# Ten experts per layer loaded in single buffers, and the last experts and the final norm reordered, in a two-layer mixture-of-experts trunk

## The chip, the core and the metric

The kernel runs on one core of one Trainium2 chip, in one launch. The metric is the device time of one execution in microseconds (us). The profile is one execution on the chip; its times count from the span's first instruction. Engines are named as in the profile: PE (TensorE; PEld is its weight load), DVE (VectorE), ACT (ScalarE), POOL (GpSimd) and SP (SyncE, which issues nearly all DMAs here).

## What is computed

Two layers on 256 tokens of width 1024, in float32. Layer 0 mixes tokens by forgetting attention, layer 1 by retention. Each is followed by a mixture of experts: a router picks 2 of 32 experts per token, and the result is added to the residual stream `h`. After layer 1 comes a last RMS norm.

```python
for i in range(DEPTH):                       # DEPTH = 2
    hn = rms_norm(h, norm_mix[i])
    h = h + (forgetting_attention if i == 0 else retention)(hn, ...)
    hn = rms_norm(h, norm_ffn[i])
    h = h + hier_moe(hn, ...)                # sum over 2 chosen experts of gate * expert(hn)
return rms_norm(h, norm_final)
# expert e: a, b = split(x @ w_gu[e]); (silu(a) * b) @ w_down[e]     w_gu[e] 1024x1024, w_down[e] 512x1024
```

Each layer reads all 32 experts' weights: 4 MiB of `w_gu` and 2 MiB of `w_down` for each, 192 MiB a layer.

## The kernel before, in words

**Stages.** `phase_a` is layer 0's attention with its router logits, `phase_moe(0, ...)` its experts, `phase_c` layer 1's retention, `phase_moe(1, ...)` its experts, and `final_norm` is a generator whose parts are run from inside the last expert.

**Weight buffers.** All large weights go through 26 slots of SBUF, 1 MiB each (128 partitions x 2048 float32). `Stream` holds a list `todo` of loads in the order of their use. `pump` issues from SP, in that order, as long as there are free slots: a load of 1 MiB takes one slot (`one`), a load of 2 MiB takes two neighbours `u` and `u ^ 1` (`two`), and where no such pair is free nothing more is issued. A slot comes free where the program calls `done` (or `give`); the DMA instruction then waits on the chip for the last reader of its slot. SP takes its instructions in order, so a load that waits holds up those behind it. `reserve` keeps slots back for buffers that the next stage will claim.

**Pieces of an expert.** `pieces(e)` says whether an expert's weights come in 1 MiB loads (four for `w_gu`, two for `w_down`) or in 2 MiB loads (two and one). Before, experts 0 to 4 (`FINE = 5`) and expert 31 come in the finer form. Expert 31's `w_down` comes in four loads of 512 KiB, one per 256 output columns (`quarter`).

**One expert.** Tokens of four experts (a group `g4`, with `e4` 0 to 3 inside it) are gathered together, 32 rows for each. `first_product` (L1037) runs four parts of 16 matmul records each (L1047); after the parts that end a load it calls `done`. For experts 29 and 30 (`WARM = 29`) each part is followed by `keep_warm(2)`: products of a matrix of ones with itself whose result nobody reads (L533). Then ACT takes the silu (L1056), DVE multiplies (L1057) and transposes (L1064), and the second product (L1075) follows, whose result DVE and ACT copy to `y4` (L1088, L1090). After `e4 == 1` `scatter_mats` prepares the group's scatter matrix; after `e4 == 2` the next group's rows are gathered (L970); at the end of a group four `scatter` products (L1101) add `y4` to the accumulators `sums[t, n]`, four PSUM banks (two halves of the tokens, two halves of the columns), which collect all groups of a layer.

**The end of a layer.** After expert 30 the program runs `keep_warm(8)` and `last_mats` (L1104: one DVE product, two transposes L1113, two thin products L1115, two DVE evictions). `last_expert` then scatters the three finished experts of the group in four products, one before and three between the parts of expert 31's first product, and runs `keep_warm(4)` after the fourth part. Second product and scatter of expert 31 go in four column pieces: `second_product(i)` (PE L1132, DVE L1135) and `scatter_piece(i)` (PE L1143), after which DVE adds the accumulator to `h` (L1145). Between them run the parts of the next stage (`between`): in layer 0 the start of `phase_c`, in layer 1 `piece(i)` of `final_norm`. The order is a string of steps, w for a second product, s for a scatter piece, b for a part of the next stage; in layer 1 it is `w0 w1 s0 w2 s1 b0 w3 s2 b1 s3 b2 b3`.

**The last norm.** `piece(i)` squares a quarter of `h` with row sums (ACT L387; for the last quarter DVE takes one of two, L385), and multiplies `h` by the gain into `fin` (POOL for quarters 0 to 2, DVE for quarter 3, L1525). After the last squares, `row_rstd` (L394 to L396) makes the factor, ACT and DVE scale the halves of `fin`, and SP stores four pieces of 256 KiB.

Of the kernel before, what the change touches and what calls it, by code (L numbers as in the profile page):

```python
# [16 lines left out]
AF = mybir.ActivationFunctionType  # L17
# [4 lines left out]
P = 128  # L22
# [8 lines left out]

FINE = 5
AHEAD = 3
# [194 lines left out]
def trunk(ctx, tc, x, fox_w_in, fox_b_f, fox_w_out, ret_w_in, ret_gn_gain, ret_w_out,  # L228
# [149 lines left out]

    def squares(i, junk, c=None, n=512, dve=False):

        c = 512 * i if c is None else c
        for t in range(2):
            a = h[:, t, c:c + n]
            if dve and t:
                V.scalar_tensor_tensor(junk[:, n:2 * n], a, 1.0, a, ALU.mult, ALU.mult, accum_out=ss[:, i, t:t + 1])  # L385
            else:
                A.activation(junk[:, 0:n], a, AF.Square, accum_out=ss[:, i, t:t + 1])  # L387

# [529 lines left out]


    def phase_moe(l, g, reserve_after, ahead, before_last, between):  # L920
        gi = 1 + 2 * l
# [144 lines left out]
        def expert(e, e4, xg, y4, after_part):  # L1066
            gg, gTt = first_product(e, e4, xg, after_part)
            turned(gg, gTt)
            by = bank("o")
            n = 4 // pieces(e)  # L1070
            for j in range(4):
                key = "wd", l, e, j // n
                w = st.get(key)
                for nb in range(4):
                    mm(by[32 * nb:32 * nb + 32, 0:256], gTt[:, 32 * j:32 * j + 32],  # L1075
                       w[:, j % n, 256 * nb:256 * nb + 256], start=j == 0, stop=j == 3, skip_group_check=True)
                if j % n == n - 1:
                    st.done(key)
                if j % 2 and e >= WARM:
                    keep_warm(2, "sc")  # L1080
            if e == 0:
                third()
                y4 = w2["y4"][0]
            for nb in range(4):
                o = y4[32 * e4:32 * e4 + 32, 256 * nb:256 * nb + 256]
                i = by[32 * nb:32 * nb + 32, 0:256]
                if nb % 2:
                    A.activation(o, i, AF.Copy)  # L1088
                else:
                    V.tensor_copy(o, i)  # L1090


        sums = {}

# [25 lines left out]
        def last_expert(xg, y4):  # L1120
            scatter(y4, 0, 96)
            gg, gTt = first_product(31, 3, xg, lambda part: scatter(y4, part + 1, 96) if part < 3 else None)
            keep_warm(4, "sc")
            turned(gg, gTt)
# [14 lines left out]
            def scatter_piece(i):  # L1139
                c = quarter(l, i)  # L1140
                for t in range(2):
                    b = sums[t, c.start // 512][:, c.start % 512:c.start % 512 + 256]
                    mm(b, w2["sm"][:, P * t:P * t + P], yd[:, i, :], start=False, stop=True, skip_group_check=True)  # L1143
                    hv = h[:, t, c]
                    V.tensor_tensor(hv, hv, b, ALU.add)  # L1145

# [14 lines left out]
        for g4 in range(8):  # L1161
            xg = g.xg if g4 % 2 == 0 else w2["xg"]
            for e4 in range(4):
# [5 lines left out]
                if e4 == 1:  # L1169
                    scatter_mats(g4)  # L1170
                if e == 2:
                    st.reserve += 2
# [5 lines left out]
                if e in ahead:  # L1178
                    before_last()
                if e == 30:  # L1180
                    keep_warm(8, "sc")
                    last_mats()
            if g4 < 7:
# [320 lines left out]
    def final_norm():  # L1504
# [14 lines left out]
        def piece(i):  # L1519
            c = quarter(1, i)  # L1520
            squares(i, junk, c.start, 256, dve=i == 3)
            if i == 3:
                row_rstd(4)
            for t in range(2):
                (G if i < 3 else V).tensor_tensor(fin[:, t, c], h[:, t, c], gain[:, c], ALU.mult)  # L1525

# [4 lines left out]
        for n in range(2):  # L1531
# [3 lines left out]
            A.activation(fin[:, 0, c], fin[:, 0, c], AF.Copy, scale=rstd[:, 0:1])  # L1535
            nc.sync.dma_start(out[0, 0:P, c], fin[:, 0, c])
        yield
# [39 lines left out]
```

## Time and profile before

| | us |
|---|---|
| median of 3 runs | 1263.21 |
| lowest and highest run | 1260.52, 1263.24 |
| the profiled execution, its own time | 1264.12 |
| its span, first to last instruction | 1262.4 |
| PE busy | 992.3 (79%) |
| DVE busy | 416.7 (33%) |
| DMA, mean over the span | 366 GB/s of 462 MB moved |

The table's busy times are sums over the whole span. The kernel has stages with different limits: PE is busy nearly all the time in the two mixer stages (about 0 to 160 us and 600 to 805 us), and the DMA engines in the two expert stages (about 172 to 600 us and 817 to 1244 us). So the stretch in which a change acts says what it is worth, not the sums. A row of a window gives, for a stretch, each engine's busy time with its number of instructions, the granted TensorE clock as a share of 2.4 GHz (0.50 is 1.2 GHz), the share of time that the 16 DMA engines were busy, and what they moved.

### The profile page before, as it was taken

What the parts mean: (1) busy time and instruction counts of PE and PEld (TensorE: products, weight loads), DVE (VectorE), ACT (ScalarE), POOL (GpSimd) and SP (SyncE); (2) the same over time, 40 slices, a digit from 0 to 9 for tenths busy, and PEclk for the clock granted to TensorE, in tenths of its full rate; (3) what the DMA queues carried; (4) which work ended last, traced back from release to release, by engine and by line L of the source; (5) the groups of instructions that cost most, each with busy time, mean ns of one, the idle gap of its engine ahead of it and who ended that gap; (6) DMA issues with size and microseconds to landing.
All of it is one profiled execution on the core that took longest, in us unless ns stands there. A gap on an engine that the chain in (4) does not pass through costs nothing. (4 is left out here: it accounts for less than half of the span.)

```text
span 1262.4 us, 21607 instructions
## 1 busy us (share of the span) xinstructions
PE 992.3 (79%) x9279; PEld 638.7 (51%) x9279; DVE 416.7 (33%) x931; ACT 317.0 (25%) x670; POOL 46.8 (4%) x55
## 2 busy tenths in 40 slices
PE   8999986777576666678999999977766666676787
PEld 8888853343232333234989888743432333233344
DVE  6776741211111111112777776421111111111113
ACT  5665521111010010101554665311110101010111
POOL 2000000000000000000223100000000000000001
PEclk9999999999797979789999999999978787877879
DMA  9966878999999999999982678779999999999994
GB/s 327 336 253 228 307 295 342 429 424 428 427 427 427 428 427 426 428 428 393 371 318 77 242 258 336 276 295 421 427 427 426 427 428 428 426 428 426 428 424 175
DMA packets 70088, 462.22 MB, mean 366 GB/s; under 512 B 8401, under 2 KB 13281, under 8 KB 41570
## 3 DMA queue, kind: packets, MB, share of 16 engines
q1 hardware_dynamic: 69568, 460.70, 90.0%
q8 instruction: 75, 1.23, 0.4%
q14 instruction: 27, 0.22, 0.0%
q10 hardware_dynamic: 418, 0.07, 0.0%
HBM read 459.70 MB, written 1.05 MB: 365 GB/s over the span
## 5 line engine op out<-in xcount | busy, mean ns | idle before, releaser
L1047 PE MATMUL sc<-slot,slot 128*32 128x256 f32 x4096 | 281.2, 426 | 57.5 <-DMA slot<-in_expert_w_gu_dram 54.2
L1047 PEld LDWEIGHTS sc<-slot,slot 128*32 128x32 f32 x4096 | 137.8, 120 | 188.4 <-issue 81.3
L1075 PE MATMUL o<-slot,slot 128*32 128x256 f32 x1984 | 145.5, 441 | 105.3 <-DMA slot<-in_expert_w_down_dram 59.6
L1075 PEld LDWEIGHTS o<-slot,slot 128*32 128x32 f32 x1984 | 72.5, 123 | 173.6 <-issue 85.6
L1057 DVE TENSOR_TENSOR slot<-slot,sc 128x128 f32<-128x128 f32 x64 | 23.8, 371 | 396.6 <-ACT slot L1056 396.6
L467 DVE SCALAR_TENSOR_TENSOR slot<-slot,gT,slot 128x512 fp32r<-128x512 f32 x160 | 125.0, 801 | 50.0 <-ACT slot L456 48.6
L500 PE MATMUL acc<-slot,slot 128*128 128x256 f32 x960 | 125.1, 287 | 0.9 <-ACT slot L456 0.4
L1090 DVE COPY slot<-o 32x256 f32<-32x256 f32 x124 | 51.8, 418 | 215.4 <-PE o L1075 188.2
L456 ACT ACTIVATE slot<-slot,gT 128x512 fp32r<-128x512 f32 x160 | 111.4, 718 | 36.2 <-PE acc L500 15.1
L500 PEld LDWEIGHTS acc<-slot,slot 128*128 128x128 f32 x960 | 118.6, 192 | 3.3 <-ACT slot L456 0.7
L1088 ACT ACTIVATE slot<-o 32x256 f32<-32x256 f32 x124 | 46.5, 375 | 292.6 <-DVE slot L1090 292.6
L1056 ACT ACTIVATE slot<-sc 128x128 f32<-128x128 f32 x64 | 17.7, 277 | 383.9 <-PE sc L1047 383.9
L512 PE MATMUL acc<-slot,slot 128*128 128x512 f32 x256 | 102.5, 400 | 0.0
L513 PE MATMUL acc<-slot,slot 128*128 128x512 f32 x256 | 100.1, 391 | 1.8 <-DVE slot L467 1.8
L514 PE MATMUL acc<-slot,slot 128*128 128x512 f32 x256 | 100.1, 391 | 0.0
L970 PE MATMUL sc<-h,slot 128*128 128x512 f32 x112 | 69.3, 778 | 33.5 <-DVE slot L959 33.5
L1101 PE MATMUL acc<-slot,slot 128*128 128x512 f32 (+1 forms) x128 | 60.9, 611 | 13.2 <-ACT slot L1088 13.2
L970 PEld LDWEIGHTS sc<-h,slot 128*128 128x128 f32 x112 | 26.5, 247 | 73.0 <-issue 73.0
L513 PEld LDWEIGHTS acc<-slot,slot 128*128 128x128 f32 x256 | 48.2, 188 | 11.6 <-DVE slot L467 2.7
L514 PEld LDWEIGHTS acc<-slot,slot 128*128 128x128 f32 x256 | 48.1, 188 | 10.2
L512 PEld LDWEIGHTS acc<-slot,slot 128*128 128x128 f32 x256 | 48.2, 188 | 9.3 <-issue 0.3
L978 DVE TENSOR_TENSOR slot<-pt,gT 128x512 f32<-128x512 f32 x28 | 19.4, 692 | 93.1 <-PE pt L977 93.1
(236 smaller groups left out, 763.2 us busy)
## 6 DMA issues: line engine op xcount, KB each, us to landing
slot<-in_expert_w_gu_dram SPq DMA_DIRECT2D x104, 2048.0 KB, 39.1
slot<-in_expert_w_down_dram SPq DMA_DIRECT2D x52, 2048.0 KB, 39.1
slot<-in_expert_w_gu_dram SPq DMA_DIRECT2D x46, 1024.0 KB, 7.5
slot<-in_ret_w_in_dram SPq DMA_DIRECT2D x24, 1024.0 KB, 14.2
slot<-in_expert_w_down_dram SPq DMA_DIRECT2D x20, 1024.0 KB, 7.7
slot<-in_fox_w_in_dram SPq DMA_DIRECT2D x15, 1024.0 KB, 13.3
slot<-in_ret_w_out_dram SPq DMA_DIRECT2D x8, 1024.0 KB, 8.8
slot<-in_fox_w_out_dram SPq DMA_DIRECT2D x4, 1024.0 KB, 15.5
```

Of the source, the lines that this page charges most:

```text
L456: A.activation(wh, w, AF.Copy, scale=1.0 if g is None else g)
L467: V.scalar_tensor_tensor(wl, w, g, wh, ALU.mult, ALU.subtract)
L500: mm(o, w[:, P * j:P * j + P], x[:, k, :], start=first and k == 0 and j % 2 == 0, stop=last and k == 7, skip_group_check=True)
L512: mm(banks[t], xh[:, q], wh, start=first and k == ks[0], stop=False)
L513: mm(banks[t], xh[:, q], wl, start=False, stop=False)
L514: mm(banks[t], xl[:, q], wh, start=False, stop=last and k == ks[-1])
L970: mm(b, o[:, t, :], h[:, t, 512 * n:512 * n + 512], start=t == 0, stop=t == 1)
L1047: mm(bgu[32 * j:32 * j + 32, 0:256].rearrange("p (two f) -> p two f", two=2), xg[:, kk, 32 * e4:32 * e4 + 32], wv[:, :, P * j:P * j + P], ...
L1075: mm(by[32 * nb:32 * nb + 32, 0:256], gTt[:, 32 * j:32 * j + 32], w[:, j % n, 256 * nb:256 * nb + 256], start=j == 0, stop=j == 3, skip_gr ...
L1088: A.activation(o, i, AF.Copy)
L1090: V.tensor_copy(o, i)
L1101: mm(sums[t, n], w2["scm"][0:rows, P * t:P * t + P], y4[0:rows, 512 * n:512 * n + 512], start=start, stop=False, skip_group_check=True)
```

## The change

- `FINE` goes from 5 to 10: experts 5 to 9 of both layers are loaded 1 MiB at a time into single slots.
- In experts 29 and 30 the second `keep_warm(2)` of the second product goes; after expert 30 `keep_warm(8)` goes, and `last_mats` moves to after expert 29.
- In `last_expert` the scatters of the finished experts stand one after each part of the first product; `keep_warm(4)` goes.
- In layer 1, after expert 24, four products of the identity with `h` add `h` to the accumulators. The DVE additions L1145 are left to layer 0. `final_norm` reads the accumulators in place of `h`: ACT squares all, DVE does all products with the gain, POOL none.
- Of the four stores of the result two are issued from ACT's queue.

```diff
--- before.py
+++ after.py
@@ -29,7 +29,7 @@
 CAP = 32
 NSLOT = 26
 
-FINE = 5
+FINE = 10
 AHEAD = 3
 
 WARM = 29
@@ -376,15 +376,10 @@
     rstd = small("rstd", 2)
 
 
-    def squares(i, junk, c=None, n=512, dve=False):
-
-        c = 512 * i if c is None else c
+    def squares(i, junk):
+
         for t in range(2):
-            a = h[:, t, c:c + n]
-            if dve and t:
-                V.scalar_tensor_tensor(junk[:, n:2 * n], a, 1.0, a, ALU.mult, ALU.mult, accum_out=ss[:, i, t:t + 1])
-            else:
-                A.activation(junk[:, 0:n], a, AF.Square, accum_out=ss[:, i, t:t + 1])
+            A.activation(junk[:, 0:512], h[:, t, 512 * i:512 * i + 512], AF.Square, accum_out=ss[:, i, t:t + 1])
 
     def row_rstd(parts=2):
 
@@ -917,6 +912,8 @@
         return g
 
 
+    hsum = {}
+
     def phase_moe(l, g, reserve_after, ahead, before_last, between):
         gi = 1 + 2 * l
         r = g.room
@@ -1076,7 +1073,7 @@
                        w[:, j % n, 256 * nb:256 * nb + 256], start=j == 0, stop=j == 3, skip_group_check=True)
                 if j % n == n - 1:
                     st.done(key)
-                if j % 2 and e >= WARM:
+                if j == 1 and e >= WARM:
                     keep_warm(2, "sc")
             if e == 0:
                 third()
@@ -1090,7 +1087,7 @@
                     V.tensor_copy(o, i)
 
 
-        sums = {}
+        sums = hsum if l else {}
 
         def scatter(y4, i, rows=P):
 
@@ -1118,9 +1115,7 @@
             V.tensor_scalar(gs, cst[:, C_NB:C_NB + 4], b[:, T:T + 1], None, ALU.mult)
 
         def last_expert(xg, y4):
-            scatter(y4, 0, 96)
-            gg, gTt = first_product(31, 3, xg, lambda part: scatter(y4, part + 1, 96) if part < 3 else None)
-            keep_warm(4, "sc")
+            gg, gTt = first_product(31, 3, xg, lambda part: scatter(y4, part, 96))
             turned(gg, gTt)
             yd = g.xg.rearrange("p (i n) q -> p i n q", i=4).rearrange("p i n q -> p i (n q)")
 
@@ -1141,8 +1136,9 @@
                 for t in range(2):
                     b = sums[t, c.start // 512][:, c.start % 512:c.start % 512 + 256]
                     mm(b, w2["sm"][:, P * t:P * t + P], yd[:, i, :], start=False, stop=True, skip_group_check=True)
-                    hv = h[:, t, c]
-                    V.tensor_tensor(hv, hv, b, ALU.add)
+                    if l == 0:
+                        hv = h[:, t, c]
+                        V.tensor_tensor(hv, hv, b, ALU.add)
 
             what = {"w": second_product, "s": scatter_piece, "b": between}
             for o in (("w0 w1 s0 s1 b0 w2 b1 s2 w3 b2 s3 b3 b4") if l == 0 else
@@ -1168,6 +1164,8 @@
                 expert(e, e4, xg, w2["y4"][g4 % 2] if e else None, start if e == 0 else lambda part: None)
                 if e4 == 1:
                     scatter_mats(g4)
+                    if g4 == 7:
+                        last_mats()
                 if e == 2:
                     st.reserve += 2
                 if e4 == 2 and g4 < 7:
@@ -1177,9 +1175,10 @@
                     st.reserve = reserve_after
                 if e in ahead:
                     before_last()
-                if e == 30:
-                    keep_warm(8, "sc")
-                    last_mats()
+                if l and e == 24:
+                    for t, n in sums:
+                        mm(sums[t, n], ident, h[:, t, 512 * n:512 * n + 512], start=False, stop=False,
+                           skip_group_check=True)
             if g4 < 7:
                 for i in range(4):
                     scatter(w2["y4"][g4 % 2], i)
@@ -1518,11 +1517,13 @@
 
         def piece(i):
             c = quarter(1, i)
-            squares(i, junk, c.start, 256, dve=i == 3)
+            hs = [hsum[t, c.start // 512][:, c.start % 512:c.start % 512 + 256] for t in range(2)]
+            for t in range(2):
+                A.activation(junk[:, 0:256], hs[t], AF.Square, accum_out=ss[:, i, t:t + 1])
             if i == 3:
                 row_rstd(4)
-            for t in range(2):
-                (G if i < 3 else V).tensor_tensor(fin[:, t, c], h[:, t, c], gain[:, c], ALU.mult)
+            for t in (1, 0):
+                V.tensor_tensor(fin[:, t, c], hs[t], gain[:, c], ALU.mult)
 
         for i in range(3):
             piece(i)
@@ -1533,7 +1534,7 @@
             V.tensor_scalar(fin[:, 1, c], fin[:, 1, c], rstd[:, 1:2], None, ALU.mult)
             nc.sync.dma_start(out[0, P:2 * P, c], fin[:, 1, c])
             A.activation(fin[:, 0, c], fin[:, 0, c], AF.Copy, scale=rstd[:, 0:1])
-            nc.sync.dma_start(out[0, 0:P, c], fin[:, 0, c])
+            A.dma_start(out[0, 0:P, c], fin[:, 0, c])
         yield
 
     g = phase_a()
```

The order in which instructions stand moves at three places. SP's queue in layer 0, from the last loads of expert 4 (the names are slots; `128x2048` fills one, `128x4096` a pair); before:

```order
L166 DMA slot_28_991<-in_expert_w_down_dram 128x2048
L166 DMA slot_25_143<-in_expert_w_down_dram 128x2048
L166 DMA slot_38_1971<-in_expert_w_gu_dram 128x4096
L166 DMA slot_39_2047<-in_expert_w_gu_dram 128x4096
L166 DMA slot_40_2057<-in_expert_w_down_dram 128x4096
L166 DMA slot_41_2102<-in_expert_w_gu_dram 128x4096
L166 DMA slot_42_2112<-in_expert_w_gu_dram 128x4096
```

and with the change:

```order
L166 DMA slot_28_991<-in_expert_w_down_dram 128x2048
L166 DMA slot_25_143<-in_expert_w_down_dram 128x2048
L166 DMA slot_8_117<-in_expert_w_gu_dram 128x2048
L166 DMA slot_4_100<-in_expert_w_gu_dram 128x2048
L166 DMA slot_5_107<-in_expert_w_gu_dram 128x2048
L166 DMA slot_29_1403<-in_expert_w_gu_dram 128x2048
L166 DMA slot_30_1405<-in_expert_w_down_dram 128x2048
L166 DMA slot_31_1431<-in_expert_w_down_dram 128x2048
L166 DMA slot_16_125<-in_expert_w_gu_dram 128x2048
L166 DMA slot_6_109<-in_expert_w_gu_dram 128x2048
```

The three loads of expert 5, each into a pair, became six, each into the next slot that comes free. Layer 1 has the same pattern.

PE in layer 1, from expert 30's second product to the second part of expert 31; before:

```order
L1075 MATMUL o<-slot_2321,slot_127 32x256 x8
L533 MATMUL sc<-ones 128x128 x2
L1075 MATMUL o<-slot_2321,slot_127 32x256 x8
L533 MATMUL sc<-ones 128x128 x10
L1113 MATMUL pt<-ident,slot_127 128x128 x2
L1115 MATMUL pt<-slot_1593,slot_127 128x1 x2
L1101 MATMUL acc<-slot_124,slot_127 128x512
L1047 MATMUL sc<-slot_125,slot_127 32x256 x8
L1101 MATMUL acc<-slot_124,slot_127 128x512
L1047 MATMUL sc<-slot_129,slot_127 32x256 x8
```

and with the change, where the lines stand three to five lower:

```order
L1072 MATMUL o<-slot_2596,slot_1405 32x256 x8
L528 MATMUL sc<-ones 128x128 x2
L1072 MATMUL o<-slot_2596,slot_1405 32x256 x8
L1044 MATMUL sc<-slot_991,slot_1405 32x256 x8
L1098 MATMUL acc<-slot_124,slot_1405 128x512
L1044 MATMUL sc<-slot_129,slot_1405 32x256 x8
```

Ten fillers, the two transposes, the two thin products and the first scatter no longer stand between the experts; the transposes and thin products now stand after expert 29's scatter matrix.

DVE in the last pieces of layer 1, from the second product of piece 2; `waits` names the engines that an instruction waits for; before:

```order
L1135 TENSOR_TENSOR slot_1593<-pt,slot_1593 128x256 [waits PE_49]
L1145 TENSOR_TENSOR h<-h,acc 128x256 [waits PE_49] x2
L1135 TENSOR_TENSOR slot_1593<-o,slot_1593 128x256 [waits PE_49]
L1145 TENSOR_TENSOR h<-h,acc 128x256 [waits PE_49] x4
L385 SCALAR_TENSOR_TENSOR slot_1595,ss<-h 128x256 [waits DMAHW7_49,DMAHW2_49,DVE_49]
L394 TENSOR_REDUCE st__85<-ss 128x2 [waits DVE_49,Activation_49]
```

and with the change:

```order
L1130 TENSOR_TENSOR slot_117<-o,slot_117 128x256 [waits PE_49]
L1526 TENSOR_TENSOR slot_1431<-acc,slot_118 128x256 [waits Activation_49]
L1526 TENSOR_TENSOR slot_1431<-acc,slot_118 128x256
L1526 TENSOR_TENSOR slot_1431<-acc,slot_118 128x256 [waits Activation_49]
L1526 TENSOR_TENSOR slot_1431<-acc,slot_118 128x256
L389 TENSOR_REDUCE st__85<-ss 128x2 [waits Activation_49]
L390 TENSOR_SCALAR st__85<-st__85 128x2 [waits DVE_49]
```

DVE no longer adds to `h`; its products with the gain read the accumulators and stand behind a wait for ACT.

## Rows read from the trace of the kernel before

**Rows 1.** The page's slices of the span, 40 equal ones: GB/s moved.
```profile
GB/s 327 336 253 228 307 295 342 429 424 428 427 427 427 428 427 426 428 428 393 371 318 77 242 258 336 276 295 421 427 427 426 427 428 428 426 428 426 428 424 175
```

**Rows 2.** Windows, layer 0 early in its experts: stretch, length, PE, PEld, DVE, ACT, POOL, PEclk, DMA, GB/s.
```profile
190.00:210.00 20.00, 14.20 (x156) 7.36 (x152) 4.43 (x10) 2.50 (x6) 0.00 (x0) 0.91 0.78 292
```

**Rows 3.** Windows, layer 1 early in its experts (same columns).
```profile
820.00:860.00 40.00, 28.97 (x357) 15.65 (x350) 9.09 (x24) 5.68 (x15) 0.00 (x0) 0.96 0.78 316
840.00:850.00 10.00, 7.28 (x32) 3.76 (x36) 2.58 (x5) 1.83 (x4) 0.00 (x0) 0.83 0.30 126
```

**Rows 4.** Timeline of SP in layer 1: start, length, queue, line, what, how many.
```profile
826.33 10.25 SPq L166 DMA_DIRECT2D slot<-in_expert_w_gu_dram  x2
850.34 0.33 SPq L166 DMA_DIRECT2D slot<-in_expert_w_down_dram  x1
```

**Rows 5.** Window in layer 1 with 1 MiB loads alone in flight (columns as in rows 2).
```profile
822.00:824.00 2.00, 2.00 (x44) 1.47 (x40) 0.25 (x1) 0.00 (x0) 0.00 (x0) 1.00 1.01 426
```

**Rows 6.** The chain that ended last, layer 1: start, length, what.
```profile
904.77 3.64 PE sc L1047 x64
...
1116.93 6.41 PE sc L970 x8
...
1165.67 39.07 DMA slot<-in_expert_w_gu_dram
...
1204.88 1.93 PE sc L1047 x16
```

**Rows 7.** Timeline of PE from expert 30 to the last pieces, layer 1.
```profile
1234.89 2.50 PE L533 MATMUL sc<-ones 128*128 128x128 f32 x20
...
1237.44 0.51 PE L1115 MATMUL pt<-slot,slot 128*128 128x1 f32 x4
...
1238.84 1.07 PE L1047 MATMUL sc<-slot,slot 128*32 128x256 f32 x16
1239.84 1.12 PE L1101 MATMUL acc<-slot,slot 96*128 96x512 f32 x2
...
1247.34 0.66 PE L1132 MATMUL sc<-slot,slot 128*32 128x64 f32 x32 [0.17 <-issue]
```

**Rows 8.** Timeline of layer 0 from expert 30's second product on, in brackets the idle time before.
```profile
580.91 1.07 PE L1075 MATMUL o<-slot,slot 128*32 128x256 f32 x16 [1.63 <-DMA slot<-in_expert_w_down_dram]
...
583.55 2.50 PE L533 MATMUL sc<-ones 128*128 128x128 f32 x20
...
587.51 1.07 PE L1047 MATMUL sc<-slot,slot 128*32 128x256 f32 x16
...
596.55 0.72 ACT L456 ACTIVATE slot<-slot,gT 128x512 fp32r<-128x512 f32 x1 [1.40 <-DMA slot<-in_ret_w_in_dram]
...
600.78 0.66 PE L1132 MATMUL pt<-slot,slot 128*32 128x64 f32 x32
```

**Rows 9.** Window at the end of layer 0's experts (columns as in rows 2).
```profile
592.00:596.00 4.00, 3.84 (x42) 1.83 (x31) 0.69 (x2) 0.28 (x1) 0.00 (x0) 1.00 1.04 351
```

**Rows 10.** Window in layer 1 where expert 24 runs (columns as in rows 2).
```profile
1100.00:1150.00 50.00, 35.86 (x346) 17.09 (x346) 7.60 (x18) 5.04 (x13) 0.00 (x0) 0.80 1.00 426
```

**Rows 11.** Timelines of PE, DVE and ACT in the last pieces of layer 1.
```profile
1251.82 1.99 PE L1143 MATMUL acc<-slot 128*128 128x256 f32 x8
...
1251.96 0.42 DVE L1135 TENSOR_TENSOR slot<-o,slot 128x256 f32<-128x256 f32 x1 [0.19 <-PE o L1132]
1252.56 1.72 DVE L1145 TENSOR_TENSOR h<-h,acc 128x256 f32<-128x256 f32 x4 [0.17 <-PE acc L1143]
...
1254.86 0.16 DVE L394 TENSOR_REDUCE st__85<-ss 128x2 f32<-128x8 f32 x1
...
1253.61 0.42 ACT L387 ACTIVATE slot<-h 128x256 f32<-128x256 f32 x1
...
1254.15 0.42 ACT L387 ACTIVATE slot<-h 128x256 f32<-128x256 f32 x1
```

**Rows 12.** Window at the start of expert 29, layer 1 (columns as in rows 2).
```profile
1205.00:1206.00 1.00, 1.00 (x12) 0.53 (x15) 0.00 (x0) 0.00 (x0) 0.00 (x0) 0.50 0.96 410
```

## The prediction

> **What bounds the kernel now.** I read the page's slices first, then windows over the two stretches where a slice is low, then SP's queue there, the chain that ended last, and the timelines of the two layer ends. In the slices the reader is to see two long plateaus at 426 to 428 GB/s, the experts of layer 0 and of layer 1: there the DMA engines set the pace and nothing else can be worth anything [rows 1]. Each plateau has a low stretch shortly after its start. In layer 0, from 190 to 210, 292 GB/s were moved [rows 2]; in layer 1, from 820 to 860, 316, and of that only 126 from 840 to 850 [rows 3]. PE idles there too, so neither engine is the limit: SP is. Its load of a pair that it began to issue at 826.33 held it until 836.58, and the next issue is at 850.34 [rows 4]. Slots came free one by one in that time, but a load of 2 MiB needs two neighbours. The chain in layer 1 agrees: it ends in a wait of 39.07 for a load, until expert 29's first product at 1204.88 [rows 6]. From there to the end PE's own work is the path [rows 7]; in layer 0 loads stay the path into the next stage [rows 8].
>
> **The change part by part.** The sum is made against the profiled execution, 1264.12; the median of the runs, 1263.21, lies 0.9 lower, and I take that off at the end.
>
> *Layer 0, experts 5 to 9 in single slots.* Each freed slot takes the next 1 MiB at once, so the low stretch fills to the plateau's rate: (428 − 292)·20/428 = **−6.4** [rows 1, 2]. The bytes are the same, and all later loads, which are back to back, move up by that.
>
> *Layer 1, the same.* (428 − 316)·40/428 = **−10.5** [rows 1, 3]; 840 to 850 alone gives 7.1 of it. That loads of 1 MiB run as fast as pairs is shown from 822 to 824, where only such loads are in flight: 426 GB/s [rows 5]. Bounds of both terms together: nothing (rivals below) and 16.9.
> Beside this row stands a rule of the Trainium skill, "DMA: Bandwidth & Descriptors", section "Anatomy of one DMA — SWDGE (gpsimd) path": a DMA costs about 2.0 us fixed plus its bytes at 436 GB/s. Paid one after another, the 30 additional loads would cost an estimated 60 by that page, and the time would end near 1301; the same section puts most of the 2 us down to the wait for completion, which loads in flight together can share, and the row agrees with that reading (these loads are SP's, not GpSimd's).
>
> *Layer 0's end.* Expert 30's second product ends near 583.55, expert 31's first part begins at 587.51: 3.96 of fillers and `last_mats` [rows 8]. But loads are late here: the second product itself waited 1.63 for one [rows 8]. So this stretch gains what the DMAs behind let it gain. With 4 MiB of `w_gu` at 428 behind that load (9.8), expert 31's first product would end near 591 in place of 592. What follows waits for `w_down` and for retention's first weights, at 351 GB/s [rows 9]: ACT's wait of 1.40 at 596.55 for such a load stays [rows 8]. Only the third piece, at 600.78, comes earlier, by my count at 598.2: **−2.5**, bounds 0 (all loads) and −3.9 (all PE).
>
> *Layer 1's end.* The fillers of 2.50 at 1234.89 and what follows up to 1238.84 go, and expert 31's first part stands directly behind expert 30's second product: **−3.9** [rows 7]. The first part carried no wait in the trace, so its weights had landed before. The first scatter now has one part, 1.07 [rows 7], to cover the copies of expert 30's result; one DVE pass over 128x256 takes 0.42 [rows 11], so that holds. The four scatters are the same four, in another place: 0.
>
> *`last_mats` behind expert 29.* It now lies on PE's path between experts 29 and 30: its DVE product, which no row times alone, then transposes and thin products. PE's share is 0.56, from 1237.39 to 1237.95 [rows 7]; the product and its hand-over are put at a DVE pass of 0.42 and a wait of 0.19 [rows 11]: **+1.2**, bounds 0.6 (DVE part hidden) and 1.6. In layer 0 it lies inside waits for loads: 0.
>
> *The last pieces.* Before, DVE's additions of 1.72 at 1252.56 and ACT's squares ran beside each other, and the row sum came at 1254.86 [rows 11]. ACT's squares come one every 0.54 (1253.61, 1254.15) [rows 11], and four of them still stand at the end, so taking the additions away by itself gains nothing. New is a wait: PE's products of pieces 2 and 3 go to the accumulator bank that DVE reads for pieces 0 and 1, and the built program makes them wait for it; DVE's product in turn waits for ACT's squares of its piece. The last scatter then starts near 1252.7 instead of within the block at 1251.82 [rows 11], and the row sum comes near 1255.05: **+0.2**, bounds −0.1 (wait already met) and +0.6.
> The Trainium skill, "PSUM — Partial Sum Buffer", section "PSUM bank collisions raise a hardware error", says that accesses of two engines to one bank and quadrant must be kept apart even at other addresses; by that rule this wait can't be dropped and the sum keeps its +0.2, where by addresses alone it would be −0.1. No row of the kernel before shows such a wait.
>
> *Costs that I put at nothing.* Four products of the identity after expert 24: of the kind of the 6.41 for eight at 1116.93 [rows 6], so at most about 6.4 if all eight's time is taken. Cover: from 1100 to 1150 PE is busy 35.86 of 50 while loads run at 426 GB/s [rows 10]; without that cover they would cost it all. The four filler records behind expert 29's second product stood beside the copies that `last_mats` is now queued behind on DVE: 0, at best −0.5 (four of the 20 that take 2.50) [rows 7]; expert 30's are counted above. The gain products that move from POOL to DVE: DVE waits for ACT there. Two stores on ACT's queue: the last issue comes at the same time, 0 to −0.2.
>
> The sum: −6.4 − 10.5 − 2.5 − 3.9 + 1.2 + 0.2 = −21.9, so 1242.2 against the profiled execution and **1241.3** as a median. The bounds of the small terms add up to −3.0 (1.4 at layer 0's end, 0.6, 0.3, 0.5, 0.2) and to +3.3 (2.5, 0.4, 0.4); I allow 2 either way for a low stretch that is not wholly filled or for loss at its edges that is saved too. Since not all of these go one way, the case spans 1237 to 1246.5.
>
> **The rivals.** *Slower: every load pays a price of its own,* so that twice as many loads move less. Retention's first weights, also 1 MiB each, ran at 351 GB/s [rows 9]. If experts 5 to 9 did, 62.9 MB (60 MiB) would take 179.2 in place of 147.0: +32.2, net +10.3, or 1273.5. It decides from 0.36 us more per load (21.9 over 60 loads; below about 373 GB/s). Against it: the 426 of the same weights [rows 5]; in the stretch of the 351 loads also waited for slots, by my reading. Chance 0.04. This is the mechanism of the page cited above, with a price from rows in place of its 2 us.
>
> *The clock falls in expert 31.* The fillers that went kept PE busy. At 1204.88, behind a wait for a load, the granted clock is 0.50 (1.2 GHz) [rows 12] and a part takes 1.93 in place of 1.07 [rows 6, 7]. Four such parts are +3.4, four scatters at twice 1.12 +4.5, the last pieces about +3: 1252. Against it: real products follow without a gap. 0.08.
>
> *The gap only moves.* From expert 10 on pairs are wanted again, and slots freed singly may again not be neighbours; if each layer lost a stretch like 840 to 850 (7.1), 14.2 would come back: 1255.5. Against it: by then more is queued than PE has read, and PE's next late point, expert 8's first product at 904.77 [rows 6], comes with the loads at 428. 0.08.
>
> *Layer 0's gain gets lost before retention*, because that stage waits for its weights or for slots: −6.4 and −2.5 fall away, 1250.2. Against it: the slots come free with the experts, which move up. 0.06.
>
> **How the numbers follow.** Forecast 0.74, rivals 0.04, 0.08, 0.08, 0.06. The range takes the forecast's own span and, above, the lost gain of layer 0, to 1250.5; the clock, the moved gap and the slower case stay outside, with 0.20 together. A measurement of this kernel tells about 0.3% (3.8 us) from no change; all cases but the slower one lie beyond that: faster 0.95, same 0.01, slower 0.04.
>
> **What would show it.** Right: windows early in both expert stages at 420 or more, with SP issuing all through; expert 31's first part directly behind expert 30's second product in layer 1; a gap of about 1.2 before expert 30; clock 1.00 from expert 30 to the end. Wrong: a new low window after expert 9, loads of 1 MiB below 373 GB/s, a clock of 0.50 in expert 31, or the last scatter more than 1 behind its second product.

## The result, and the profile after

The changed kernel takes 1248.28 us (median of 4 runs, 1246.19 to 1251.0) against 1263.22 before: a ratio of 0.9887 with a 95% interval of 0.9861 to 0.9914. On the chip of a later set it took 1246.43 (1245.63 to 1246.9) against 1263.14, 0.9868 [0.985 to 0.9886]. So it is faster by 15 to 17 (1.1 to 1.3%); 21.9 was forecast. Both medians lie in the range, 1237 to 1250.5; the first lies above the 1246.5 at which the forecast's own terms end.

The slices of the page of the changed kernel answer to [rows 1]:

```profile
GB/s 339 321 264 192 321 279 421 419 427 426 427 426 427 428 428 426 427 426 394 378 335 69 268 237 308 332 357 419 423 427 428 427 427 427 427 427 427 428 424 192
```

The dip at the start of each plateau is gone: 421 and 419 stand where 342 and 429 stood in layer 0, 357 and 419 for 295 and 421 in layer 1 (the slice with 357 holds the first 20 us of the experts, which move 349 GB/s, 364 before). The same stretches as in [rows 2, 3] in windows (columns as there):

```profile
190.00:210.00 20.00, 14.20 (x187) 7.78 (x182) 4.44 (x10) 2.50 (x6) 0.00 (x0) 1.00 1.01 420
820.00:860.00 40.00, 29.86 (x338) 15.67 (x334) 8.02 (x19) 5.41 (x14) 0.00 (x0) 0.91 1.01 419
840.00:850.00 10.00, 9.05 (x72) 4.71 (x75) 1.38 (x2) 1.19 (x2) 0.00 (x0) 0.85 1.02 421
...
300.00:550.00 250.00, 164.44 (x1788) 80.03 (x1780) 37.40 (x91) 24.05 (x64) 0.00 (x0) 0.87 1.01 427
```

The first three rows are full, yet 420 and not 427 as in the fourth, a stretch where pairs are loaded. SP in layer 1, beside [rows 4]; a row of this view joins several issues, and its length runs from the first to the end of the last, with SP's waits between them:

```profile
821.69 4.37 SPq L166 DMA_DIRECT2D slot<-in_expert_w_gu_dram  x4
826.60 3.86 SPq L166 DMA_DIRECT2D slot<-in_expert_w_down_dram  x2
831.84 5.29 SPq L166 DMA_DIRECT2D slot<-in_expert_w_gu_dram  x4
839.28 9.28 SPq L166 DMA_DIRECT2D slot<-in_expert_w_down_dram  x2
849.10 1.19 SPq L166 DMA_DIRECT2D slot<-in_expert_w_gu_dram  x2
```

So SP still has a pause: of the two loads in the row at 839.28 the second is issued at 848.24. But the DMA engines don't run dry in it, for more was queued ahead: 10 MiB from 821.69 to 837.13, where the kernel before issued 6 MiB from 822.88 to 836.58. Its row at 826.33 in [rows 4] is also two issues, each of 0.33, the second at 836.25, with a wait between them.

PE's timeline in layer 1, from expert 29 to the last scatter, answers to [rows 7]:

```profile
1193.22 1.07 PE L1044 MATMUL sc<-slot,slot 128*32 128x256 f32 x16 [1.54 <-DMA slot<-in_expert_w_gu_dram]
...
1207.68 0.41 PE L1031 MATMUL pt<-ident,slot 128*128 128x128 f32 x2 [1.95 <-DVE slot L1028]
1208.70 0.66 PE L1110 MATMUL pt<-ident,slot 128*128 128x128 f32 x2 [0.61 <-DVE slot L1106]
1209.15 0.85 PE L1112 MATMUL pt<-slot,slot 128*128 128x1 f32 x4
1209.93 3.77 PE L1514 MATMUL sc<-slot,ones 1*128 1x512 f32 x4
1213.63 1.94 PE L1044 MATMUL sc<-slot,slot 128*32 128x256 f32 x16
...
1224.72 1.07 PE L1072 MATMUL o<-slot,slot 128*32 128x256 f32 x16
1225.61 1.05 PE L1044 MATMUL sc<-slot,slot 128*32 128x256 f32 x16
1226.74 1.13 PE L1098 MATMUL acc<-slot,slot 96*128 96x512 f32 x2
...
1238.72 2.41 PE L1138 MATMUL acc<-slot 128*128 128x256 f32 x8
```

Expert 31 (1225.61) starts directly behind expert 30's second product, as forecast. Ahead of expert 30, PE waits 1.95 for DVE's product of the scatter matrix and 0.61 for that of `last_mats`; then the gain products (of the final norm's gain, spread over the partitions by PE) take 3.77 and the first two parts of expert 30 1.94 each. The windows show the granted clock there: 0.50 (1.2 GHz), in layer 1 and also around expert 30 of layer 0:

```profile
1210.00:1213.60 3.60, 3.60 (x4) 1.08 (x4) 0.57 (x2) 0.60 (x1) 0.00 (x0) 0.50 0.97 410
570.00:576.00 6.00, 5.93 (x42) 3.37 (x42) 0.57 (x2) 0.00 (x0) 0.00 (x0) 0.50 1.01 425
```

In layer 1 a part of this is not new. The kernel before, at the same place:

```profile
1219.64 0.41 PE L1034 MATMUL pt<-ident,slot 128*128 128x128 f32 x2 [1.30 <-DVE slot L1031]
1219.98 2.40 PE L1515 MATMUL sc<-slot,ones 1*128 1x512 f32 x4
1222.31 1.94 PE L1047 MATMUL sc<-slot,slot 128*32 128x256 f32 x16
```

Its first two parts of expert 30 took 1.94 too. The wait of 1.30 became 1.95 because the filler records in front of it went, which costs nothing. New in layer 1 are the wait of 0.61, the transposes and thin products of `last_mats`, and 1.37 in the gain products; in layer 0, where the parts of expert 30 took 1.07 before, the half clock is new.

The timelines cut the span at five places: the first product of each layer's experts, expert 29's first product and expert 31's first part in layer 1, and the end. Where the time went, in us against the kernel before; the last two columns are experiments of the next section:

| stretch | before | forecast | changed | changed, second profile | only `FINE` | all but `FINE` |
|---|---|---|---|---|---|---|
| start to layer 0's experts | 172.30 | 0 | +1.31 | −0.64 | −0.91 | −0.86 |
| layer 0's experts and retention | 644.60 | −8.9 | −5.09 | −6.49 | −2.94 | −0.16 |
| layer 1's experts up to 29 | 387.98 | −10.5 | −7.88 | −7.91 | −8.76 | +1.82 |
| experts 29 and 30 | 33.96 | −2.7 | −1.57 | −2.65 | −0.78 | −1.44 |
| expert 31 to the end | 23.56 | +0.2 | −0.27 | −0.31 | −0.41 | −0.46 |
| span | 1262.4 | −21.9 | −13.5 | −18.0 | −13.8 | −1.1 |

The first profile of the changed kernel is the highest of its four runs (1251.0, the lowest 1246.19), and that of all but `FINE` the highest of six (1263.44, the median 1258.7), so these two columns understate their kernels. What the table's first row shows lies ahead of all that the change touches.

### The profile page after: what moved, and what is told of

The parts are those of the page before. It is cut to its first block, busy times and chain, and to the rows that moved or that the text cites. A ratio compares the mean times of both kernels' runs of the same rounds, so it can differ in the third digit from the quotient of the medians.

```text
span 1248.9 us, 21544 instructions
## 1 busy us (share of the span) xinstructions
PE 982.5 (79%) x9223; PEld 634.3 (51%) x9223; DVE 414.3 (33%) x927; ACT 317.6 (25%) x672; POOL 42.8 (3%) x49
## 4 chain that ended last, share of the span: by engine, by line
DMA 49%; PE 29%; DVE 2%; issue 1%; ACT 1%; POOLq 0%; ACTq 0%; SPq 0%; DVEq 0%
DMA slot<-in_expert_w_gu_dram 29%; DMA slot<-in_expert_w_down_dram 19%; PE sc L1044 5%; PE acc L495 4%; PE acc L509 3%; PE acc L507 3%; PE acc L508 3%; PE o L1072 3%; PE sc L967 1%; PE acc L1098 1%; DMA slot<-in_ret_w_in_dram 1%; DVE slot L1087 1%; PE pt L528 0%; PE acc L1138 0%; ACT slot L1085 0%
## 5 line engine op out<-in xcount | busy, mean ns | idle before, releaser
L1044 PE MATMUL sc<-slot,slot 128*32 128x256 f32 x4096 | 277.4, 422 | 54.9 <-DMA slot<-in_expert_w_gu_dram 51.8
L1072 PE MATMUL o<-slot,slot 128*32 128x256 f32 x1984 | 137.8, 422 | 101.4 <-DMA slot<-in_expert_w_down_dram 58.7
L967 PE MATMUL sc<-h,slot 128*128 128x512 f32 x112 | 72.8, 811 | 33.5 <-DVE slot L956 33.5
## 6 DMA issues: line engine op xcount, KB each, us to landing
slot<-in_fox_w_out_dram SPq DMA_DIRECT2D x4, 1024.0 KB, 14.6
```

What stands on the lines that cost most here:

```text
L967: mm(b, o[:, t, :], h[:, t, 512 * n:512 * n + 512], start=t == 0, stop=t == 1)
L1044: mm(bgu[32 * j:32 * j + 32, 0:256].rearrange("p (two f) -> p two f", two=2), xg[:, kk, 32 * e4:32 * e4 + 32], wv[:, :, P * j:P * j + P], ...
```

## The experiments

Two theories were set against each other for the missing part (other letters below are those of the expectation above them). P: the lead of the loads is there, and PE loses it between experts 29 and 30. L: the loads never gained what the windows said. Ratios are to the kernel before on the same chip.

**One part alone.** `FINE = 10` in the kernel before, and the changed kernel with `FINE = 5`:

```diff
-FINE = 5
+FINE = 10
```

> Only FINE = 10 of the change, in the kernel before. Theory P (PE's path between experts 29 and 30 eats the lead): the loads get about 3.5 us ahead in layer 0 and 8.5 more in layer 1; with the fillers and last_mats as they were, most of it arrives: expert 29's first product in layer 1 some 11 to 12 us earlier than in the kernel before, the whole 9 to 12 faster, about 1252. Rival L (the loads gain less than the windows say, because 1 MiB loads are slower or the slots come late): layer 0's lead is gone by expert 29, the whole 5 to 8 faster, about 1256.

> The change without FINE = 10: only the reordered ends and the final norm. Theory P: expert 31 starts 4 earlier behind expert 30 in both layers; between experts 29 and 30 last_mats costs about 2 in layer 1, while in layer 0 waits for loads (2.7 in the kernel before) hide it; the whole 3 to 6 faster, about 1258. Rival L: the ends give all that the change gives beyond 5 to 8, so 7 to 10 faster, about 1254. Theory C (the fillers that went cost clock): expert 29 and 30 run at half the clock for more of their parts than in the kernel before, and the gain is below 3.

`FINE` alone: 1250.31 against 1264.95, 0.9897 [0.9881 to 0.9913], which is nearly all of the gain and more than the 9 to 12 of P. The rest alone: 1258.7, 0.995 [0.9936 to 0.9965]. By the medians the two parts give 14.6 and 6.3, together more than the 15 to 17 of the whole. With `FINE` alone expert 29 of layer 1 starts 12.6 earlier, as P has it; but in layer 0 only 2.94 of the 6.4 arrive. There PE still waits for a load, and the clock falls behind the wait. PE, only `FINE`, layer 0, expert 30:

```profile
571.62 1.07 PE L1047 MATMUL sc<-slot,slot 128*32 128x256 f32 x16
...
575.72 1.93 PE L1075 MATMUL o<-slot,slot 128*32 128x256 f32 x16 [2.39 <-DMA slot<-in_expert_w_down_dram]
...
578.71 1.07 PE L1075 MATMUL o<-slot,slot 128*32 128x256 f32 x16
```

The product starts 5.2 earlier than in [rows 8] (580.91), but it and its fillers take 1.35 more at a clock of 0.50, so that expert 31's start is only 3.84 earlier (583.67 against 587.51).

In the profile of the kernel with all but `FINE` the dip is deeper than before, and layer 1 up to expert 29 takes 1.82 more. The second 20 us from the first expert product of layer 0 and of layer 1, first in the kernel before, then in this run:

```profile
192.30:212.30 20.00, 14.02 (x144) 7.27 (x144) 4.58 (x11) 2.59 (x6) 0.00 (x0) 0.91 0.79 299
836.90:856.90 20.00, 14.02 (x144) 7.26 (x144) 4.58 (x11) 2.59 (x6) 0.00 (x0) 0.91 0.57 214
...
191.44:211.44 20.00, 14.20 (x157) 7.50 (x152) 4.43 (x10) 2.50 (x6) 0.00 (x0) 0.91 0.70 267
835.88:855.88 20.00, 14.19 (x156) 7.32 (x150) 4.44 (x10) 2.50 (x6) 0.00 (x0) 0.91 0.52 184
```

I read it so that the order in which neighbouring slots come free hangs on the whole program, and a change elsewhere moves the dip as long as pairs are wanted; that was not tried by itself, and it is a single profile. So the two parts can't be added up from these two runs.

**The same kernel again.**

> The changed kernel as it is, beside the others of this set on one chip. Theory P: layer 0's experts start near 171.4 as in the four runs so far, not at 173.6 as in its first profile, since that start has nothing to do with the change; 1247 to 1250 against 1265. Rival S (the change makes layer 0's experts start 1 to 2 later): the start is near 173.6 again.

1246.43, with the experts of layer 0 starting at 171.66: the 173.61 of the first profile was one execution's. Rival S falls. In this profile expert 30 of layer 0 ran at the full clock behind the same waits:

```profile
565.25 0.41 PE L1031 MATMUL pt<-ident,slot 128*128 128x128 f32 x2 [1.94 <-DVE slot L1028]
566.27 0.41 PE L1110 MATMUL pt<-ident,slot 128*128 128x128 f32 x2 [0.61 <-DVE slot L1106]
...
566.95 1.07 PE L1044 MATMUL sc<-slot,slot 128*32 128x256 f32 x16
```

So that clock is not the same in each execution; it makes part of the spread of the runs.

**The price of a 1 MiB load.** All experts in such loads (`FINE = 32`):

> The changed kernel with all experts in loads of 1 MiB. Theory R (each 1 MiB load costs a little more than half a pair: 420 GB/s early in the experts against 427 later): the whole plateau runs at 420, 277 MB more at that rate, about 11 slower than the changed kernel, near 1259. Rival Q (the 420 belongs to the start of a layer, not to the size): 427 in the middle of the layer, within 2 of the changed kernel.

```profile
300.00:550.00 250.00, 170.91 (x1764) 74.48 (x1764) 36.46 (x88) 23.81 (x63) 0.00 (x0) 0.83 1.01 421
```

421 in the middle of the layer, where pairs gave 427; 1253.93, 0.9931 [0.9914 to 0.9948], 7.5 slower than the changed kernel beside it. R holds and Q falls, though the 11 were too many: 252 loads of experts 10 to 30 make 264 MB, and at 421 for 427 that is 8.8. Each 1 MiB load costs 2.49 where half a pair costs 2.46, about 0.035 more.

**The place of `last_mats`.** Back behind expert 30, without fillers:

```diff
-                    if g4 == 7:
-                        last_mats()
...
+                if e == 30:
+                    last_mats()
```

> The changed kernel with last_mats back after expert 30 (without fillers there). Theory P: 1.8 per layer come back between experts 29 and 30, but PE now waits for DVE's product between 30 and 31, 2 to 3 per layer: 0 to 3 slower than the changed kernel, 1249 to 1251. Rival L: PE is not the path there in layer 0, so layer 0 changes by less than 1 and the whole by 1 or less either way.

1252.14, 0.9904 [0.9889 to 0.9919]: 2 to 5 behind the changed kernel by its two ratios. PE now waits in front of expert 31, and in layer 1 the clock falls there:

```profile
1221.58 0.58 PE L1110 MATMUL pt<-ident,slot 128*128 128x128 f32 x2 [1.95 <-DVE slot L1106]
1221.96 0.85 PE L1112 MATMUL pt<-slot,slot 128*128 128x1 f32 x4
1222.74 1.93 PE L1044 MATMUL sc<-slot,slot 128*32 128x256 f32 x16
1224.60 2.08 PE L1098 MATMUL acc<-slot,slot 96*128 96x512 f32 x2
```

Expert 31 to the end takes 25.86 here (1222.74 to 1248.6), 23.25 in the changed kernel's second profile. So the profiles say that the move of `last_mats` pays; the interval overlaps that of the changed kernel's first set and lies just above that of the second. The other way, everything that PE waits for moved ahead by one more expert:

```diff
-                if e4 == 1:
+                if e4 == (0 if g4 == 7 else 1):
                     scatter_mats(g4)
                     if g4 == 7:
                         last_mats()
...
-        phase_moe(1, g, 3, (22, 29), lambda: next(fin), lambda i: next(fin))
+        phase_moe(1, g, 3, (22, 28), lambda: next(fin), lambda i: next(fin))
```

> The changed kernel with expert 31's matrices, the last group's scatter matrix and the gain products all after expert 28 in place of 29, where PE waits nearly 3 us for a load in both layers. Theory P: PE no longer waits between experts 29 and 30 (4.2 us from the end of 29's second product to the gain products, and those take 3.8 at half the clock in layer 1); layer 0 returns up to the 3.5 that its loads are ahead, layer 1 another 3 to 5: 5 to 8 faster than the changed kernel, 1240 to 1243, and expert 30's parts take 1.07 rather than 1.94. Rival L: expert 30 then waits for its loads as long as it waited for DVE before: less than 2 faster, 1246 to 1248.

> The version with the matrices and the gain products after expert 28 once more, on the chip of this set: 0.984 of the kernel before again, within 0.002; were its lead over the changed kernel the luck of one chip, 0.987 or more.

1243.7, 0.984 [0.9826 to 0.9854], and again 1243.88, 0.9843 [0.9826 to 0.986]. It beats the kernel before. Over the changed kernel it is 3 to 6 ahead by the ratios, at the low end of P's 5 to 8; the two never ran on the same chip, and its intervals lie below that of the changed kernel's first set and overlap that of the second. PE in layer 1, the first of the two:

```profile
1187.51 0.41 PE L1031 MATMUL pt<-ident,slot 128*128 128x128 f32 x2 [1.82 <-DVE slot L1028]
...
1189.76 3.77 PE L1514 MATMUL sc<-slot,ones 1*128 1x512 f32 x4
1193.46 1.94 PE L1044 MATMUL sc<-slot,slot 128*32 128x256 f32 x16
...
1204.55 1.07 PE L1072 MATMUL o<-slot,slot 128*32 128x256 f32 x16
1205.44 1.05 PE L1044 MATMUL sc<-slot,slot 128*32 128x256 f32 x16
...
1214.46 1.07 PE L1072 MATMUL o<-slot,slot 128*32 128x256 f32 x16 [1.64 <-DMA slot<-in_expert_w_down_dram]
...
1216.99 1.05 PE L1044 MATMUL sc<-slot,slot 128*32 128x256 f32 x16
```

The wait, the gain products and the half clock now lie where PE waited for expert 29's load; expert 30 follows expert 29 at once (1205.44), and loads are late again (1.64). From the first product of layer 1's experts to expert 31 it takes 407.17, the changed kernel's second profile 411.38. That is P's mechanism for layer 1. In layer 0 P's gain did not come: experts and retention take 638.14 here and 638.11 in that profile. With the gain products moved further, behind expert 25:

> As the version before it in this set, with the gain products after expert 25 instead of 28. Theory P (with the waits for DVE gone, loads set the end again): the 3.8 of the gain products go from PE's path at expert 29, but experts 29 to 31 then wait for loads: 0 to 2 faster. Rival D (PE is still the path from expert 29 on): 3 to 5 faster.

1243.38, 0.984 [0.9822 to 0.9857], no difference that the interval can tell. Experts 29 to 31 now wait for loads; experts 29 and 30:

```profile
1199.93 1.07 PE L1072 MATMUL o<-slot,slot 128*32 128x256 f32 x16 [1.04 <-DMA slot<-in_expert_w_down_dram]
...
1205.17 1.93 PE L1044 MATMUL sc<-slot,slot 128*32 128x256 f32 x16 [2.53 <-DMA slot<-in_expert_w_gu_dram]
```

So loads bound that version, and rival D falls.

**The clock.** Six products of ones in the wait behind expert 29, and in another kernel the fillers of the second half back:

```diff
+                    if g4 == 7:
+                        keep_warm(6, "sc")
                     scatter_mats(g4)
```

```diff
-                if j == 1 and e >= WARM:
+                if j % 2 and e >= WARM:
```

> The changed kernel with six more products of ones behind expert 29's second product, where PE waits 1.95 us for DVE. Theory C (the wait is what drops the clock): the granted clock stays at 1.00, the gain products take 2.0 in place of 3.77 in layer 1, expert 30's first two parts 1.07 in place of 1.94 in both layers; 1.5 to 3 per layer, as far as loads allow: 2 to 5 faster than the changed kernel. Rival T (the thin products of last_mats and of the gain drop it, not the wait): the clock is 0.50 from last_mats on as before, and the time is the same within 1.5.

> The changed kernel with the fillers behind the second half of the second products of experts 29 and 30 put back. Theory P: behind expert 29 they stand beside the wait for DVE (1.94) and cost nothing; behind expert 30 they delay expert 31 by 0.5 per layer: 0 to 1.5 slower than the changed kernel. Theory C (their absence let the clock fall): expert 30's first parts take 1.07 and the kernel is 1 to 3 faster.

The first: 1244.92, 0.9854 [0.9833 to 0.9875]; the wait is 0.42 in place of 1.94, and the gain products run at the full clock, but expert 30 then falls to half within its first parts:

```profile
1206.03 0.41 PE L1031 MATMUL pt<-ident,slot 128*128 128x128 f32 x2 [0.42 <-DVE slot L1028]
...
1207.73 1.98 PE L1516 MATMUL sc<-slot,ones 1*128 1x512 f32 x4
1209.64 1.53 PE L1044 MATMUL sc<-slot,slot 128*32 128x256 f32 x16
1212.25 1.68 PE L1044 MATMUL sc<-slot,slot 128*32 128x256 f32 x16
```

Half of what C expected for PE, and 1.5 in the time, which the intervals don't separate. The second: 1249.25, 0.988 [0.9861 to 0.99], in line with P; its gain products take 3.77 again, so the missing fillers did not make that clock. Nor does the length of the first wait settle it: here it is 1.31, with the 0.61 behind it, while in the run with `last_mats` behind expert 30 a first wait of 1.94 without a second left the gain products at 1.98 (1205.82). Which of the waits and thin products lets the clock fall is not separated.

**The last norm.** `h` added by DVE again (so the four products with `h` are out too), squares and gain products of `h`, POOL's share and all stores on SP as before:

> The changed kernel with h added by DVE after each piece and with the old final norm and stores. Theory P (the accumulator reads cost a wait that balances what they save): within 1 of the changed kernel, the last scatter near the second product before it and the row sum 0.2 earlier, the end 0 to 0.4 later. Rival N (the norm in the accumulators is worth more than 1 because DVE's additions and POOL were on the path): 1 to 2 slower.

1245.0, 0.9858 [0.9836 to 0.9879]. From expert 31's first part (1219.97) to the end (1243.2) it takes 23.23; the changed kernel's second profile has 23.25. The new norm is worth nothing either way; N falls. The 1.4 between the medians, which the intervals don't separate, lies ahead of expert 31: 1.0 of it in layer 1 up to expert 29 (379.09 against 380.07).

**How many experts need single slots.** `FINE = 7` in the version with the matrices after expert 28:

> The version with matrices and gain after expert 28, and only experts 5 and 6 in addition in 1 MiB loads (FINE = 7). Theory G (the gap is the wait of the first pairs while slots come free singly): the gap comes back behind expert 6, smaller than for FINE = 5: 3 to 10 slower than with FINE = 10. Rival R (two experts are enough to queue ahead, and each 1 MiB load costs 0.04 us more than its share of a pair): no gap, 0.5 to 1.5 faster.

1245.56, 0.9851 [0.983 to 0.9871]. The dip is back, later and smaller:

```profile
220.00:230.00 10.00, 7.54 (x102) 3.94 (x106) 1.09 (x3) 0.48 (x2) 0.00 (x0) 0.83 0.93 362
850.00:860.00 10.00, 6.67 (x64) 3.21 (x60) 0.84 (x2) 0.75 (x2) 0.00 (x0) 1.00 0.54 224
```

G's mechanism is shown, its price was too high: 1.7 between the medians, and the intervals overlap.

## Why the prediction was right, and where it was not

**What bounds the kernel, and the two dips: right.** The loads that want pairs were the cause. `FINE` alone brings most of the gain, the windows fill, and no new dip comes behind expert 9: the rival of the moved gap fell, and `FINE = 7` shows that it would have been right for fewer experts. Two things are less than the prediction says. SP has a pause in the changed kernel too; what changed is how much is queued before it. And every run that takes away the pairs also halves the loads: none tried 2 MiB into any two slots, so that the slots must be neighbours is argued, not shown.

**The range: luck in part.** The first median, 1248.28, is above the 1246.5 of the forecast's own span. It lies in the range because that was widened to 1250.5 for the case that layer 0's gain is lost, and this case did not come: −5.09 to −6.49 arrived.

**The size of the two terms: too large.** Forecast −6.4 and −10.5. Counted from each kernel's own first expert product, the changed kernel's second profile has 2.4 MB more landed after 40 us in layer 0 and 4.0 MB in layer 1, sums over windows of 20 us; at 427 that is 5.7 and 9.4. Over the next 40 us it gives back 0.3 MB in each layer (0.75), because 1 MiB loads run at 420. Hence −5.0 and −8.7. The step that failed is "fills to the plateau's rate": I took the plateau of the pairs. The 426 of [rows 5], two microseconds long, did not show the difference. At 0.035 for each of the 60 loads an estimated 2.1 of the 3.2 missing go back to this; the rest lies at the edges of the windows. The slower rival's mechanism does exist, with 0.035 per load against the 0.36 from which it would decide. On this point stands the Trainium skill, "DMA: Bandwidth & Descriptors", section "Anatomy of one DMA — SWDGE (gpsimd) path", with about 2 us fixed for each DMA on GpSimd's path. On SP's queue the runs show 0.07 for each additional load (two of 0.035 in place of one pair): loads in flight together share nearly all of it.

**Layer 0's end: forecast −2.5 on top, to be handed on whole.** Layer 0 with retention gave −5.09 and −6.49 for −8.9; 1.4 of the missing is the term above. I put `last_mats` at 0 there, "inside waits for loads". At the full clock that holds. In the second profile expert 30 still waits for a load behind it, expert 31 waits for loads again, and the third piece starts at 593.65 (600.78 before):

```profile
576.30 1.07 PE L1072 MATMUL o<-slot,slot 128*32 128x256 f32 x16 [2.66 <-DMA slot<-in_expert_w_down_dram]
```

There 1.0 of the forecast is missing, and why stays open; moving the matrices ahead did not bring it (638.14). At the half clock the 0 does not hold. In the first profile no wait for a load is left in expert 30, and PE takes 30.9 from expert 29 to the end of expert 30's second product (552.65 to 583.58) where it had taken 27.1 (556.48 to 583.55); 1.4 of this is left at the end of the layer, between the two profiles. The lead of the loads is not what used up the cover, for with `FINE = 5` (all but `FINE`) expert 30 goes the same way:

```profile
573.71 1.93 PE L1044 MATMUL sc<-slot,slot 128*32 128x256 f32 x16
...
583.73 1.07 PE L1072 MATMUL o<-slot,slot 128*32 128x256 f32 x16 [0.57 <-DVE slot L1061]
```

From its first part to its second product it takes 10.02 without a wait for a load, in the changed kernel's second profile 9.35 with one of 2.66 (566.95 to 576.30). I had priced the cover at the full clock alone.

**`last_mats` behind expert 29: +1.2 forecast.** From DVE's scatter matrix to the gain products PE takes 1.84 in the first profile (1208.09 to 1209.93) and 1.30 in the second (1205.00 to 1206.30), of which 0.61 is a wait: DVE's product comes behind the scatter matrix's transposes. So the term was right at the full clock, and 0.2 above its upper bound where the clock fell. The half clock of the gain products (3.77 for 2.40) adds 1.4, which I had not counted at all. That experts 29 and 30 still gave −2.65 for −2.7 in the second profile is two things against each other: the second part of expert 30, at half the clock before, took 1.13 there. Against the price of `last_mats` stands the wait at the other place, which the profile with `last_mats` behind expert 30 shows to be dearer.

**Expert 31: −3.9 forecast, right.** Expert 30's last product to expert 31's first part is 0.89 (1224.72 to 1225.61), before 4.95 (1233.89 to 1238.84): −4.06. The clock in expert 31 stayed at 1.00 in both profiles, and that rival falls; where PE waits directly in front of expert 31, as with `last_mats` behind expert 30, it does fall (0.50 from 1222.74 to 1228.40). What fell in the changed kernel was the clock ahead of expert 30 and in it. So the sign "clock 1.00 from expert 30 to the end" failed.

**The last pieces: +0.2 forecast.** From the first column piece to the row sum: 7.52 before, 7.57 now. The new wait is there: the last scatters take 2.41 in place of 1.99, as PE waits 0.5 for DVE's product from the same bank:

```profile
1239.19 0.74 DVE L1526 TENSOR_TENSOR slot<-acc,slot 128x256 f32<-128x256 f32 x2
...
1241.80 0.16 DVE L389 TENSOR_REDUCE st__85<-ss 128x2 f32<-128x8 f32 x1 [0.52 <-ACT slot L1522]
```

ACT's squares cover it but for 0.05, and expert 31 to the end came out at −0.27 and −0.31 for +0.2. The last scatter starts 1.2 behind the end of its second product (1239.99, 1238.78; 0.8 before), more than the 1 that I had named as a sign of being wrong, and the end does not feel it. Keeping to the Trainium skill's rule on one bank ("PSUM — Partial Sum Buffer", "PSUM bank collisions raise a hardware error") thus costs PE 0.4 and the end next to nothing; no run leaves the wait out. The four products with `h`, the stores and POOL's work cost and gained nothing that the runs tell, as forecast; the products with `h` were not tried alone.

Two steps, then, were off in the same direction: the rate of 1 MiB loads, and the clock after PE's waits, which cost layer 0 its cover in one profile and layer 1 its gain products in both. In the second profile 3.2 are missing in the two terms, 1.0 at layer 0's end and 0.8 between the loads' lead in layer 1 and expert 29, and 0.5 came on top at the last pieces. The first profile adds 1.4 in layer 0, 1.1 at experts 29 and 30 and 2.0 ahead of all that the change touches. How often the clock falls behind such a wait, and so how the runs of one kernel spread, stays open.

## What to carry to other kernels

Loads of two buffers can leave the DMA engines idle while buffers come free one by one; small loads at the start of such a stage cured it here, and cost 1.5% of the rate while they last, so use them only until the queue is ahead. When new work is to hide behind waits for loads, ask whether it still does at half the clock: here it did at the full clock and not at the half. Put PE's waits for another engine where PE would wait for a load anyway: in layer 1 that gave 4.2 us by the profiles (3 to 6 in all by ratios from different chips) beyond the change here.

## What the runs showed that I had not expected

A load of 1 MiB among its like runs at 420 to 421 GB/s, one of 2 MiB at 427, steadily over 250 us. And a wait of PE is paid twice when the clock falls behind it: after 1.95 and 0.61 of waiting, four gain products took 3.77 in place of 1.98; with 0.42 for 1.95 they took 1.98, and so they did after one wait of 1.94 alone. The same two waits left the clock at 1.00 in layer 0 in one profile of this kernel and at 0.50 in another.
